# A two-layer attention backbone: attention probabilities transposed by VectorE and DMA through a DRAM scratch

## The chip, the core and the metric

The kernel runs on one core of a Trainium2 chip. The metric is the device time of one execution in microseconds, from from its first to its last instruction with what lies around them. The core's engines work side by side, each through its own queue in order: TensorE (matrix products; in the profile PE for matmuls and PEld for its weight loads), VectorE (DVE), ScalarE (ACT), GpSimd (POOL), and SyncE (SP), which here only issues DMA transfers.

## The reference, cut to what matters

Two layers work on 512 latent tokens and 256 context tokens of width 1024. Layer 0 is differential attention with eight heads; layer 1 is grouped-query attention with eight query heads and two key/value heads.

```python
def sweep_attention(q, k, v):        # for each block of 128 queries
    s = jnp.einsum('bqhgd,bkhd->bhgqk', qblk.astype(jnp.float32), k32) * scale
    p = jax.nn.softmax(s, axis=-1)
    return jnp.einsum('bhgqk,bkhd->bqhgd', p.astype(v.dtype), v)
...
o1 = sweep_attention(qq[..., 0, :], kk[..., 0, :], vv)      # layer 0
o2 = sweep_attention(qq[..., 1, :], kk[..., 1, :], vv)
o = o1 - lam.astype(o1.dtype) * o2
...
o = sweep_attention(qq, kk, vv)                             # layer 1
```

Latent queries read all 768 keys (latent and context). Context queries, in layer 0 alone, read the 256 context keys. Around the attention stand RMS norms, modulation by a condition vector, rotary positions, projections with weights of 1024 columns and gates. The result is the latent stream after both layers, in 32-bit floats.

## The kernel before, in words

**Precision by splitting.** TensorE's products take operands of the type fp32r. To keep 32-bit precision each operand is split into a high part (a copy that rounds to fp32r, on ScalarE) and a low part (the source minus the high part, on VectorE or GpSimd), and each product is three matmuls: high by high, high by low, low by high (`mm3`, line 537).

**Attention, by pairs.** Queries are worked in tiles of 128. A unit (`unit` in `s_units`, line 1267, and in `s1_units`, line 1852) does one tile of one head: TensorE puts 128 x 768 scores into PSUM, VectorE takes the row maximum, ScalarE the exponential with its row sum, VectorE the reciprocal, and GpSimd scales the row (tile `p`). In layer 0 there are two score maps for each tile, and VectorE subtracts the second with `scalar_tensor_tensor`. Two units form a pair, a chunk of 256 queries: two chunks (0 and 1) for each of eight heads in each layer are over latent queries, and layer 0 has a third chunk (2) for each head over context queries.

**The turn.** The product with V needs keys on the partitions, so the probabilities have to be transposed. In `tstep` (lines 1346 and 1879) TensorE transposes blocks of 128 x 128 against the identity matrix, four to a PSUM bank: two key blocks of two query tiles. ScalarE copies the bank into `ah` (high), and VectorE subtracts it from the bank into `al` (low). Three such steps cover 768 keys. In `mstep` (lines 1360 and 1892) `pv_mm` (line 542) runs six matmuls for each step: V's high and low parts stationary, `ah` and `al` moving, 256 columns each. `ah` and `al` have `AB = 3` buffers (line 74). In layer 0 the tile `p` has six buffers, in layer 1 five.

**V and K.** V's projection (`v_mm`, line 1038; `proj_tok`, line 1560, which also serves K and Q of layer 1) has the tokens as its stationary operand, 128 consecutive columns of the activation tiles `hhi`/`hlo` or `h1hi`/`h1lo`, and weights moving, so V comes out with tokens on the partitions. Keys lie with features on the partitions and tokens along the free dimension; `qk_split_` (line 1182) and `k_tr` (line 1739) split them.

**The order of the work.** The program is traced twice. A planner (class `Plan`) first records every operation and its dependences, prices each with constants, and schedules all five queues by list scheduling (`schedule`, line 290): at each step the operation that can start first, ties by priority. Then the program is emitted with exactly these orders, so each queue's order is fixed before the run. For a DMA the planner computes (lines 336 to 338):

```python
go = s + (330 if e == "SP" else 450)
dma = max(dma, go + 300) + op.cost / 350.0
end = max(go + 1700 + op.cost / 350.0, dma) + (800 if op.cost == 131072 else 300)
```

Here `s` is when the queue reaches it, in nanoseconds, and `op.cost` its bytes. Priorities follow from steps with lags (`chunk`, line 763): a transposing step is due 7.0 us (`LA`, line 53) behind its pair's last unit, and its PV step 4.5 us (`LM`, line 73) behind the transposing step. Between these steps the planner fills TensorE with projections of later heads.

**DMA.** SyncE issues weight loads (`wsplit`, line 606) into two `raw` buffers, each 512 KB; ScalarE and GpSimd or VectorE split them. ScalarE's queue issues the small swaps for the rotary positions.

Of the kernel before, what the change touches and what calls it, by code (L numbers as in the profile page):

```python
# [8 lines left out]
F32 = mybir.dt.float32  # L9
# [6 lines left out]
P = 128  # L16
# [31 lines left out]
WBUFS = 3  # L48
XE = [2, 2, 2, 2, 3, 3]
# [24 lines left out]
AB = 3  # L74
MEM = 227168
AHEAD_OPS = 1500
MARGIN = 1.08
SLOT = {}
# [28 lines left out]
class Plan:  # L107


    def __init__(self, mem, psum, sizes):  # L110
        self.mem, self.sizes = mem, sizes
        self.psum = dict(psum)
        self.banks = {t.tensor.name: t.free_size() for t in psum.values()}
        self.width = mem.shape[1]
        self.ops, self.offs, self.tail, self.seen = [], [0], None, {}
        self.marks = []
        self.pools, self.stack = [], {"left": [], "right": []}
        for q in QUEUE:
            setattr(self, q, Queue(self.add, QUEUE[q]))


    def pool(self, name, side="left", psum=False):
        return Pool(self, name, side, psum)

# [41 lines left out]
    def add(self, q, meth, args, kw):  # L166
# [14 lines left out]
        for aps_, w in ((ins, 0), (outs, 1)):  # L181
            for ap in aps_:
                if ap.space == bass.MemoryType.DRAM:
                    continue
                name, spans, parts = self.places(ap)
                if name not in self.banks:
# [103 lines left out]
    def schedule(self, rank):  # L290
# [15 lines left out]
        while len(order) < count:  # L306
# [79 lines left out]
class Emit:  # L386
# [7 lines left out]
    def add(self, eng, meth, args, kw):  # L394
        self.ops.append(getattr(eng, meth)(*args, **kw))  # L395
        return self.ops[-1]

# [81 lines left out]
def tile_backbone(  # L479
# [30 lines left out]
    ps1 = ctx.enter_context(pl.pool("ps1", psum=True))  # L510

# [24 lines left out]

    def mm3(o, ahi, alo, bhi, blo, start, stop):
# [4 lines left out]
    def pv_mm(o, vh, vl, c, ah, al, kt, first, last):  # L542
        terms = [(v, a, e) for v, a in ((vh, ah), (vl, ah), (vh, al)) for e in range(2)]
        for i, (v, a, e) in enumerate(terms):
            nc.tensor.matmul(o, v[:, kt + e, c], a[:, e * 256:e * 256 + 256], start=first and i == 0, stop=last and i == 5)
# [577 lines left out]
    with pl.pool("t0") as t0:  # L1123
# [58 lines left out]
        def qk_split_(h, rr, eng=nc.gpsimd):  # L1182
            qk[h] = tuple(t0.tile([P, T], F32R, tag=f"qk{i}", name=nm("qk"), bufs=1) for i in range(4))
            for r, hi, lo in ((rr[0], *qk[h][:2]), (rr[1], *qk[h][2:])):
                nc.scalar.copy(hi, r)
                eng.tensor_tensor(lo, r, f32(hi), ALU.subtract)
# [77 lines left out]
        def s_units(h, qts):  # L1264
            res = []

            def unit(qt):
# [11 lines left out]
                prev = None  # L1279
                for j in range(nk // w):  # L1280
                    c = slice(k0 + j * w, k0 + j * w + w)
                    for i, (a, b) in enumerate(((qh, kh_), (qh, kl_), (ql, kh_))):
                        for m in (1, 0):
                            r = slice(m * 64, m * 64 + 64)
                            with after(prev), chained(prev):
                                prev = nc.tensor.matmul(
                                    sc[m][:, j if nk == T else m, :w], a[r, tok], b[r, c], start=i == 0, stop=i == 2)
                for m in range(2):
# [3 lines left out]
                    pt = t0.tile([P, T], F32, tag=f"p{m}", name=nm("p"), bufs=6 if m == 0 else 2)[:, :nk]  # L1292
                    pv_ = pt.rearrange("p (j n) -> p j n", j=2) if nk == T else pt
                    nc.scalar.activation(pv_, scv, AF.Exp, bias=mx, accum_out=l[:, m:m + 1])
# [5 lines left out]
                    else:  # L1300
                        nc.vector.tensor_tensor(r, r, nlam, ALU.mult)
                        nc.vector.scalar_tensor_tensor(ps_[0], pt, r, ps_[0], ALU.mult, ALU.add)
                        res.append(ps_[0])

            def unit_ctx():
# [3 lines left out]
                for qt in (NQ, NQ + 1):  # L1309
                    tok = slice(qt * P, (qt + 1) * P)  # L1310
                    for i, (a, b) in enumerate(((qh, kh_), (qh, kl_), (ql, kh_))):
                        for m in (1, 0):
                            r = slice(m * 64, m * 64 + 64)
                            with after(prev), chained(prev):
                                prev = nc.tensor.matmul(
                                    sc[m][:, qt - NQ, :C], a[r, tok], b[r, S:T], start=i == 0, stop=i == 2)
                l = [small(2), small(2)]
                pts = []
                for m in range(2):
                    mx = small(2)  # L1320
                    nc.vector.tensor_reduce(mx, sc[m][:, :, :C], AX.X, ALU.max, negate=True)
                    pt = t0.tile([P, T], F32, tag=f"p{m}", name=nm("p"), bufs=6 if m == 0 else 2)
# [19 lines left out]
        def pv_steps(h, at, ch, after, ts, ms):  # L1342
            kts = range(6) if ch < 2 else range(4, 6)
            st = {}

            def tstep(kt):
                tr = trp()
                for e in range(2):
                    j = kt + e - kts[0]
                    for i, a in enumerate(at):  # L1350
                        nc.tensor.transpose(tr[:, e * 256 + i * P:e * 256 + (i + 1) * P], a[:, j * P:(j + 1) * P], ident)
# [4 lines left out]
                nc.scalar.copy(ah, tr)  # L1356
                nc.vector.tensor_tensor(al, tr, f32(ah), ALU.subtract)
                st[kt] = ah, al

            def mstep(kt):  # L1360
# [6 lines left out]
                pv_mm(o, vh, vl, vc, ah, al, kt, kt == kts[0], kt == kts[-2])  # L1367
                if kt == kts[-2]:
# [5 lines left out]
                    nc.scalar.copy(gT[h][:, sl], o)  # L1374
# [185 lines left out]
    def proj_tok(o, w, t):  # L1560
        sl = slice(t * P, (t + 1) * P)
        for kt in range(KT):
            wh, wl = w[kt // 4]
            c = slice((kt % 4) * 256, (kt % 4) * 256 + 256)
            mm3(o, h1hi[:, kt, sl], h1lo[:, kt, sl], wh[:, c], wl[:, c], kt == 0, kt == KT - 1)
# [127 lines left out]
    with pl.pool("t1", "right") as t1p:  # L1693
# [45 lines left out]
        def k_tr(m, kr):  # L1739
# [4 lines left out]
            sl = slice(m * P, (m + 1) * P)  # L1744
            nc.scalar.copy(kh[:, :, sl], tv)
            nc.vector.tensor_tensor(kl[:, :, sl], tv, f32(kh[:, :, sl]), ALU.subtract)
# [15 lines left out]
        for what, m in KV:  # L1762
# [7 lines left out]
            else:  # L1770
# [3 lines left out]
                run(proj_tok(o, wk if what == "k" else wv, m))  # L1774
# [74 lines left out]
        def s1_units(h, ms):  # L1849
            res = []  # L1850

            def unit(m):
# [4 lines left out]
                for j in range(2):  # L1857
                    c = slice(j * 384, j * 384 + 384)
                    mm3(sc[:, j, :384], qa[:, sl], qb[:, sl], kh[:, g, c], kl[:, g, c], True, True)
# [6 lines left out]
                pt = t1q.tile([P, T], F32, tag="p", name=nm("p"), bufs=5)  # L1866
                l = small()
                nc.scalar.activation(pt.rearrange("p (j n) -> p j n", j=2), scv, AF.Exp, scale=sr, bias=nmx, accum_out=l)
                nc.vector.reciprocal(l, l)
                scaled(EN1, pt, pt, l)  # L1870
                res.append(pt)
# [3 lines left out]
        def pv1_steps(h, at, ch, after, ts, ms):  # L1875
            g = h // 4
            st = {}

            def tstep(kt):
                tr = trp()  # L1880
                for e in range(2):
                    for i, a in enumerate(at):
                        nc.tensor.transpose(tr[:, e * 256 + i * P:e * 256 + (i + 1) * P], a[:, (kt + e) * P:(kt + e + 1) * P], ident)
# [4 lines left out]
                nc.scalar.copy(ah, tr)  # L1888
                nc.vector.tensor_tensor(al, tr, f32(ah), ALU.subtract)
                st[kt] = ah, al  # L1890

            def mstep(kt):
# [5 lines left out]
                pv_mm(o, vh, vl, c, ah, al, kt, kt == 0, kt == 4)  # L1898
                if kt == 4:
                    if ch == 0:  # L1900
                        gT1[h] = t1p.tile([P, 512], F32, tag="g1", name=nm("g1"), bufs=8)
                    (nc.scalar.copy if EG1 == "a" else nc.vector.tensor_copy)(gT1[h][:, ch * 256:ch * 256 + 256], o)
# [217 lines left out]
```

## Time and profile before

| what | us |
| --- | --- |
| median of 3 runs (809.27 to 809.84) | 809.46 |
| the profiled execution's own time | 808.79 |
| its span, first to last instruction | 807.0 |
| TensorE busy (97% of the span) | 786.4 |
| VectorE, ScalarE, GpSimd busy | 473.6, 482.0, 437.4 |
| bytes moved by DMA: 77.78 MB, mean 96 GB/s | |

How to read the rows that follow. A row of a group names the line, the engine, the operation, output <- inputs by the program's names, the shapes and the count; behind the bar stand busy microseconds, mean nanoseconds of one, and the idle time ahead of it with what ended it. Nearly all instructions carry line 395, a helper that emits them, so tiles and operations tell them apart. A row of windows is: stretch, its length, then busy time and count of PE, PEld, DVE, ACT and POOL, the granted TensorE clock, the mean busy share of 16 DMA engines, and GB/s. A row of waits is: who, for whom, microseconds in total, times, longest. A row of DMA issues is: tile <- source, queue, count, KB each, median microseconds from issue to landing. A row of the timeline is: start, length, engine, operation and how many were merged.

### The profile page before, as it was taken

What the parts mean: (1) busy time and instruction counts of PE and PEld (TensorE: products, weight loads), DVE (VectorE), ACT (ScalarE), POOL (GpSimd) and SP (SyncE); (2) the same over time, 40 slices, a digit from 0 to 9 for tenths busy, and PEclk for the clock granted to TensorE, in tenths of its full rate; (3) what the DMA queues carried; (4) which work ended last, traced back from release to release, by engine and by line L of the source; (5) the groups of instructions that cost most, each with busy time, mean ns of one, the idle gap of its engine ahead of it and who ended that gap; (6) DMA issues with size and microseconds to landing.
All of it is one profiled execution on the core that took longest, in us unless ns stands there. A gap on an engine that the chain in (4) does not pass through costs nothing.

```text
span 807.0 us, 14385 instructions
## 1 busy us (share of the span) xinstructions
PE 786.4 (97%) x5482; PEld 699.8 (87%) x5482; DVE 473.6 (59%) x824; ACT 482.0 (60%) x1083; POOL 437.4 (54%) x512
## 2 busy tenths in 40 slices
PE   7899999999999999999999999999999999999997
PEld 5779888889887898797989998898999899898886
DVE  3425787774847546656546743788346455655625
ACT  5524577684565645666538843784466676768622
POOL 4545776874585654757923312366887646644101
PEclk9899999999999999999999999999999999999999
DMA  9951120132142431323430152035321200201112
GB/s 302 363 180 67 65 75 31 40 108 89 40 158 79 144 105 53 105 80 96 165 106 27 62 227 79 1 89 175 120 70 53 96 11 27 79 27 55 51 53 105
DMA packets 41541, 77.78 MB, mean 96 GB/s; under 512 B 3584, under 2 KB 18688, under 8 KB 41472
## 3 DMA queue, kind: packets, MB, share of 16 engines
q1 hardware_dynamic: 38048, 71.71, 27.4%
q10 hardware_dynamic: 3424, 5.15, 1.8%
q8 instruction: 43, 0.70, 0.4%
q14 instruction: 26, 0.21, 0.1%
HBM read 70.56 MB, written 2.10 MB: 90 GB/s over the span
## 4 chain that ended last, share of the span: by engine, by line
PE 91%; DVE 3%; ACT 2%; DMA 2%; issue 1%; SPq 0%; POOL 0%; ACTq 0%; DVEq 0%; POOLq 0%
PE bk L395 75%; PE sc L395 16%; DMA ag<-in_ada_w 1%; DMA raw<-in_post_g 1%; DVE gacc L395 1%; DMA gw<-in_ada_w 0%; ACT whi L395 0%; SPq L395 0%; DVE h L395 0%; ACT sq L395 0%; DVE hf L395 0%; ACT p L395 0%; DVE sw L395 0%; DVE gate L395 0%; ACT jk L395 0%
## 5 line engine op out<-in xcount | busy, mean ns | idle before, releaser
L395 PE MATMUL bk<-whi,h 128*128 128x256 f32 (+1 forms) x1184 | 244.6, 299 | 2.0 <-DVE kn L395 1.3
L395 PE MATMUL bk<-h,whi 128*128 128x512 f32 (+2 forms) x832 | 225.6, 351 | 0.0
L395 POOL TENSOR_TENSOR wlo<-raw,whi 128x256 fp32r<-128x256 f32 x200 | 162.5, 839 | 76.7 <-ACT whi L395 75.3
L395 PEld LDWEIGHTS bk<-whi,h 128*128 128x128 f32 x1184 | 191.0, 189 | 14.6 <-issue 4.9
L395 PE MATMUL bk<-wlo,h 128*128 128x256 f32 (+1 forms) x592 | 176.5, 299 | 0.0
L395 PEld LDWEIGHTS bk<-h,whi 128*128 128x128 f32 x832 | 144.1, 188 | 16.5 <-issue 4.4
L395 PE MATMUL bk<-h,wlo 128*128 128x512 f32 (+2 forms) x416 | 145.7, 351 | 0.0
L395 DVE TENSOR_REDUCE sm<-sc 128x1 f32<-128x768 f32 (+2 forms) x114 | 101.0, 897 | 25.7 <-PE sc L395 25.4
L395 PEld LDWEIGHTS bk<-wlo,h 128*128 128x128 f32 x592 | 111.7, 189 | 4.8 <-issue 1.4
L395 POOL TENSOR_SCALAR p<-p,sm 128x768 f32<-128x768 f32 (+1 forms) x80 | 68.4, 858 | 77.6 <-DVE sm L395 72.8
L395 DVE TENSOR_TENSOR al<-bk,ah 128x512 fp32r<-128x512 f32 x104 | 69.4, 685 | 39.3 <-ACT ah L395 38.8
L395 ACT CAST whi<-raw 128x1024 fp32r<-128x1024 f32 (+1 forms) x70 | 71.7, 1026 | 31.9 <-PE bk L395 27.7
L395 ACT ACTIVATE p<-sc,sm 128x768 f32<-128x768 f32 (+1 forms) x96 | 72.9, 762 | 21.6 <-DVE sm L395 15.6
L395 ACT CAST ah<-bk 128x512 fp32r<-128x512 f32 x104 | 59.0, 590 | 43.5 <-PE bk L395 43.1
L395 PEld LDWEIGHTS bk<-h,wlo 128*128 128x128 f32 x416 | 78.4, 188 | 7.5 <-issue 1.3
L395 PE MATMUL bk<-ident,p 128*128 128x128 f32 x416 | 64.3, 275 | 1.6 <-DVE ql L395 1.1
L395 PEld LDWEIGHTS bk<-ident,p 128*128 128x128 f32 x416 | 49.0, 141 | 11.4 <-issue 2.0
L395 DVE SCALAR_TENSOR_TENSOR p<-p,sm,p 128x768 f32<-128x768 f32 (+1 forms) x48 | 53.4, 1120 | 3.3 <-POOL p L395 0.5
L395 ACT ACTIVATE jk<-bk 128x128 f32<-128x128 f32 (+4 forms) x66 | 22.7, 345 | 53.5 <-PE bk L395 34.4
L395 POOL TENSOR_TENSOR sz<-sz,za 128x384 f32<-128x384 f32 (+1 forms) x24 | 29.4, 1227 | 40.3 <-ACT za L395 39.7
L395 PE MATMUL sc<-qk,qk 64*128 64x384 f32 (+1 forms) x480 | 50.6, 341 | 0.0
L395 DVE RECIPROCAL sm<-sm 128x1 f32<-128x1 f32 (+1 forms) x114 | 18.1, 159 | 52.0 <-ACT p L395 51.5
(191 smaller groups left out, 1375.5 us busy)
## 6 DMA issues: line engine op xcount, KB each, us to landing
raw<-in_a_w SPq DMA_DIRECT2D x30, 512.0 KB, 3.5
araw<-in_ada_w SPq DMA_DIRECT2D x12, 1024.0 KB, 5.3
raw<-in_b_w SPq DMA_DIRECT2D x20, 512.0 KB, 3.5
ag<-in_ada_w SPq DMA_DIRECT2D x32, 256.0 KB, 6.5
raw<-in_w_out SPq DMA_DIRECT2D x16, 512.0 KB, 3.6
sw<-qr ACTq DMA_DIRECT2D x32, 128.0 KB, 2.1
gw<-in_ada_w SPq DMA_DIRECT2D x8, 512.0 KB, 4.1
xt<-in_x SPq DMA_DIRECT2D x4, 512.0 KB, 5.1
```

Source lines behind the costliest of these rows:

```text
L395: self.ops.append(getattr(eng, meth)(*args, **kw))
```

## The change

Chunks 0 and 1 in both layers are turned another way; the context chunk keeps TensorE's transposes. Both units of a pair write their probabilities into one tile `pp` of 1536 elements in each partition, interleaved in runs of 32. VectorE transposes all its 32 x 32 blocks in place with one instruction. Then SyncE stores the tile to a DRAM scratch and loads it back with four transfers that bring the blocks to the right partitions (tile `at`), and ScalarE and VectorE split `ah` and `al` from there, in SBUF. A pair has two buffers of `pp` and two of `at`; `ah` and `al` go from three buffers to two, and the tile `p0` of layer 0 from six of 768 to two of 512.

In the turned tile a partition holds other keys than before: latent tokens t with equal t mod 4, context tokens with equal t mod 2 go together. So V's projections take their stationary tokens with a step of 4 or 2 elements (`keys`), keys are stored permuted (`ordered`, `by_a`) with one more copy and subtraction for each head, context scores read permuted runs of 32 (`by_k`), and PV's moving operand and its output are viewed in runs of 64 and 32. The planner learns of the scratch, prices every DMA issue at 450 ns and adds `DPAD = 500` ns to each landing.

```diff
-AB = 3
+AB = 2
+P0B = 2
+ATB = 2
+PPB = 2
+DRSPLIT = 1
+DRB = 6
+PEWAY = ((), ())
...
-                go = s + (330 if e == "SP" else 450)
+                go = s + 450
                 dma = max(dma, go + 300) + op.cost / 350.0
-                end = max(go + 1700 + op.cost / 350.0, dma) + (800 if op.cost == 131072 else 300)
+                end = max(go + 1700 + op.cost / 350.0, dma) + (800 if op.cost == 131072 else 300) + DPAD
...
+    def keys(src, t):
+        if t < NQ:
+            return src[:, :S].rearrange("p (x k) -> p k x", k=4)[:, t]
+        return src[:, S:].rearrange("p (x k) -> p k x", k=2)[:, t - NQ]
...
+            if moved:
+                d, b = by_a(o, 64), a.rearrange("p (b e x) -> p e b x", b=4, e=2)[:, e]
+            else:
+                d, b = o, a[:, e * 256:e * 256 + 256]
+            nc.tensor.matmul(d, v[:, kt + e, c], b, start=first and i == 0, stop=last and i == 5)
...
+    def turn(pool, pp):
+        flat = pp.rearrange("p b u x -> p (b u x)")
+        nc.vector.transpose(flat, flat)
+        at = pool.tile([P, 4, 384], F32, tag="at", name=nm("at"), bufs=ATB)
+        for lo in range(0, 4, 4 // DRSPLIT):
+            n = 4 // DRSPLIT
+            dr = drp.tile([P // DRSPLIT, 4 * 384], F32, tag="dr", name=nm("dr"), bufs=DRB)
+            nc.sync.dma_start(dr[:, :], flat[32 * lo:32 * (lo + n), :])
+            for q in range(n):
+                nc.sync.dma_start(at[:, lo + q, :], dr[32 * q:32 * q + 32, :].rearrange("j (a c) -> a j c", a=4))
+        return at
+
+    def dma_way(layer, h, ch):
+        return (h, ch) not in PEWAY[layer]
+
+    def split_at(ah, al, src, moved):
+        hi, lo = (by_a(ah, P), by_a(al, P)) if moved else (ah, al)
+        nc.scalar.copy(hi, src)
+        nc.vector.tensor_tensor(lo, src, f32(hi), ALU.subtract)
...
-            sl = slice(t * P, (t + 1) * P)
...
-            mm3(o, hhi[kt][:, sl], hlo[kt][:, sl], wh[:, c], wl[:, c], first and kt == 0, last and kt == KT - 1)
+            mm3(o, keys(hhi[kt], t), keys(hlo[kt], t), wh[:, c], wl[:, c], first and kt == 0, last and kt == KT - 1)
...
                 ah = t0.tile([P, 512], F32R, tag="ah", name=nm("ah"), bufs=AB)
-                nc.scalar.copy(ah, tr)
-                nc.vector.tensor_tensor(al, tr, f32(ah), ALU.subtract)
+                split_at(ah, al, at[0][:, :, kt * 64:kt * 64 + P] if moved else tr, moved)
```

More of the change, by code (lines that the diff above doesn't have):

```diff
@@ L48 @@
 WBUFS = 3
+MEM = 227168
+AHEAD_OPS = 1500
+MARGIN = 1.08
+DPAD = 500
+SLOT = {}
 XE = [2, 2, 2, 2, 3, 3]
@@ L123, in pool, with scratch, dram @@
         return Pool(self, name, side, psum)
+    def scratch(self):
+        self.tile = lambda *args, **kw: self.dram()
+        return nullcontext(self)
+    def dram(self):
+        self.turns += 1
+        return self.drams[(self.turns - 1) % len(self.drams)]
     @contextmanager
@@ L182, in add @@
             for ap in aps_:
-                if ap.space == bass.MemoryType.DRAM:
+                far = ap.space == bass.MemoryType.DRAM
+                if far and all(ap.tensor.name != d.tensor.name for d in self.drams):
                     continue
-                name, spans, parts = self.places(ap)
-                if name not in self.banks:
+                name, spans, parts = (ap.tensor.name, [(0, 2048)], 1) if far else self.places(ap)
+                if name not in self.banks and not far:
                     at = spans[0][0]
@@ L1264, in s_units @@
         def s_units(h, qts):
-            res = []
+            res, pair = [], {}
             def unit(qt):
@@ L1284, in unit @@
                             r = slice(m * 64, m * 64 + 64)
+                            o = sc[m][:, j if nk == T else m, :w]
+                            if moved:
+                                b_ = b[r, j * w:j * w + w]
+                            elif nk == T:
+                                o, b_ = k_a_j(o), by_k(b[r, :], 6)[:, 3 * j:3 * j + 3]
+                            else:
+                                o, b_ = k_a_j(o), by_k(b[r, :], 2)
                             with after(prev), chained(prev):
-                                prev = nc.tensor.matmul(
-                                    sc[m][:, j if nk == T else m, :w], a[r, tok], b[r, c], start=i == 0, stop=i == 2)
+                                prev = nc.tensor.matmul(o, a[r, tok], b_, start=i == 0, stop=i == 2)
+                if nk == T and qt % 2 == 0:
+                    pair[qt // 2] = t0.tile([P, 24, 2, 32], F32, tag="pp", name=nm("pp"), bufs=PPB)
                 for m in range(2):
@@ L1302, in unit @@
                         nc.vector.scalar_tensor_tensor(ps_[0], pt, r, ps_[0], ALU.mult, ALU.add)
-                        res.append(ps_[0])
+                        if not moved:
+                            res.append(ps_[0])
+                        elif qt % 2:
+                            res.append(turn(t0, pair[qt // 2]))
             def unit_ctx():
@@ L1344, in pv_steps @@
             st = {}
+            moved = ch < 2 and dma_way(0, h, ch)
             def tstep(kt):
[L1347 to L1351, printed above, removed]
+                if not moved:
+                    tr = trp()
+                    for e in range(2):
+                        for i, a in enumerate(at):
+                            src = a[:, (kt + e - kts[0]) * P:(kt + e - kts[0] + 1) * P]
+                            nc.tensor.transpose(tr[:, e * 256 + i * P:e * 256 + (i + 1) * P], src, ident)
                 if h == 0 and ch == 0 and kt == 0:
@@ L1564, in proj_tok @@
             c = slice((kt % 4) * 256, (kt % 4) * 256 + 256)
-            mm3(o, h1hi[:, kt, sl], h1lo[:, kt, sl], wh[:, c], wl[:, c], kt == 0, kt == KT - 1)
+            a, b = (keys(t_[:, kt, :], t) if perm else t_[:, kt, sl] for t_ in (h1hi, h1lo))
+            mm3(o, a, b, wh[:, c], wl[:, c], kt == 0, kt == KT - 1)
             yield 3 * 256 / 2400.0
@@ L1743, in k_tr @@
             tv = tr[:, :256].rearrange("p (j n) -> p j n", j=2)
-            sl = slice(m * P, (m + 1) * P)
-            nc.scalar.copy(kh[:, :, sl], tv)
-            nc.vector.tensor_tensor(kl[:, :, sl], tv, f32(kh[:, :, sl]), ALU.subtract)
+            kd = [t.rearrange("p g (a n) -> p g a n", a=4) for t in (kh, kl)]
+            k = 4 if m < NQ else 2
+            for b in range(1 if m < NQ else 2):
+                a, c = (m, slice(0, P)) if m < NQ else (2 * (m - NQ) + b, slice(P, 192))
+                hi, lo = (t[:, :, a, c].rearrange("p g (k j) -> p g k j", k=k) for t in kd)
+                src = tv[:, :, b * 64:b * 64 + 32 * k].rearrange("p g (j k) -> p g k j", k=k)
+                nc.scalar.copy(hi, src)
+                nc.vector.tensor_tensor(lo, src, f32(hi), ALU.subtract)
         def k_rope(m, o, r):
@@ L1773, in tile_backbone @@
                 o = pj(256)
-                run(proj_tok(o, wk if what == "k" else wv, m))
+                run(proj_tok(o, wk if what == "k" else wv, m, what == "v"))
                 if late:
@@ L1865, in unit @@
                 nc.scalar.activation(nmx, mx, AF.Copy, scale=sr)
-                pt = t1q.tile([P, T], F32, tag="p", name=nm("p"), bufs=5)
+                if m % 2 == 0:
+                    pair[0] = t1q.tile([P, 24, 2, 32], F32, tag="pp", name=nm("pp"), bufs=PPB)
+                if moved:
+                    pt = unit_view(pair[0], m % 2)
+                    pv_, src = pt.rearrange("p (j b) x -> p j b x", j=2), scv.rearrange("p j (b x) -> p j b x", x=32)
+                else:
+                    pt = unit_row(pair[0], m % 2)
+                    pv_, src = pt.rearrange("p (j n) -> p j n", j=2), scv
                 l = small()
-                nc.scalar.activation(pt.rearrange("p (j n) -> p j n", j=2), scv, AF.Exp, scale=sr, bias=nmx, accum_out=l)
+                nc.scalar.activation(pv_, src, AF.Exp, scale=sr, bias=nmx, accum_out=l)
                 nc.vector.reciprocal(l, l)
                 scaled(EN1, pt, pt, l)
-                res.append(pt)
+                if not moved:
+                    res.append(pt)
+                elif m % 2:
+                    res.append(turn(t1q, pair[0]))
             return res, [Step(lambda m=m: unit(m), 0.97) for m in ms]
@@ L1877, in pv1_steps @@
             st = {}
+            moved = dma_way(1, h, ch)
             def tstep(kt):
[L1880 to L1883, printed above, removed]
+                if not moved:
+                    tr = trp()
+                    for e in range(2):
+                        for i, a in enumerate(at):
+                            src = a[:, (kt + e) * P:(kt + e + 1) * P]
+                            nc.tensor.transpose(tr[:, e * 256 + i * P:e * 256 + (i + 1) * P], src, ident)
                 if h == 0 and ch == 0 and kt == 0:
@@ L2107 @@
             mem = mp.tile([P, MEM // 4], F32, name="mem")[:]
+            drams = [drp.tile([P // DRSPLIT, 4 * 384], F32, name=f"dr{i}")[:, :] for i in range(DRB)]
             sizes, pl = None, None
             while pl is None or sizes != pl.sizes:
-                pl = Plan(mem, psum, sizes)
+                pl = Plan(mem, psum, drams, sizes)
                 tile_backbone(pl, *args)
```

85 lines of the change are left out of this document (59 added, 26 removed).

## The prediction, as it was put on record

> **What bounds the kernel now.** I read the busy shares first, then the chain that ended last, then what TensorE waited for, then the two attention stretches by windows.
>
> ```profile
> PE 786.4 (97%) x5482; PEld 699.8 (87%) x5482; DVE 473.6 (59%) x824; ACT 482.0 (60%) x1083; POOL 437.4 (54%) x512
> ...
> PE 91%; DVE 3%; ACT 2%; DMA 2%; issue 1%; SPq 0%; POOL 0%; ACTq 0%; DVEq 0%; POOLq 0%
> ```
> ```profile
> PE sc L395 <- POOL xt L395: 2.5, 1, 2.5
> PE bk L395 <- DVE al L395: 1.8, 2, 1.4
> ```
> ```profile
> 83.00:262.00 179.00, 178.91 (x1243) 153.27 (x1242) 125.68 (x197) 114.97 (x244) 121.66 (x118) 1.00 0.23 74
> 262.00:440.00 178.00, 177.60 (x1281) 156.29 (x1281) 104.61 (x183) 106.88 (x228) 101.41 (x102) 1.00 0.30 97
> 593.00:745.00 152.00, 149.85 (x1046) 140.78 (x1046) 83.53 (x159) 105.18 (x244) 93.02 (x117) 1.00 0.15 49
> ```
>
> TensorE is 97% busy and carries 91% of the chain; its longest single wait is 2.5 us, and for split probabilities (al) it waits 1.8 us in the whole run. Layer 0's attention runs from 83 to 440 us, layer 1's from 593 to 745. In both TensorE has no gap, VectorE is 65% and 55% busy, and the sixteen DMA engines average 0.27 and 0.15. So an instruction that leaves TensorE there shortens the run, as long as nothing else comes later than it does now.
>
> **What the change removes.** The transposes of probabilities:
>
> ```profile
> L395 PE MATMUL bk<-ident,p 128*128 128x128 f32 x416 | 64.3, 275 | 1.6 <-DVE ql L395 1.1 <-DVE al L395 0.4
> ```
> ```profile
> 639.99 0.60 PE L395 MATMUL bk<-ident,p 128*128 128x128 f32 x4
> ...
> 642.06 0.40 PE L395 MATMUL bk<-ah,vh 128*128 128x256 f32 x2
> ```
>
> The 275 ns is a latency; four in a row take 0.60 us, so one follows another after (0.60 - 0.275) / 3 = 0.108 us. Eight heads, two layers, two chunks of 256 queries, twelve transposes each: 384 go (the context chunk keeps 32). That is 384 x 0.108 = **41.5 us**, half of it, 20.7, in each layer. The matmuls that stay are taken at their pace of now (256 columns: 0.12 us), except those in the third point below.
>
> **What it adds, where something already covers it.** VectorE turns 32 pairs, 1536 elements in each partition. No such instruction is in the trace; the nearest rows are one-input instructions:
>
> ```profile
> L395 DVE TENSOR_REDUCE sm<-sc 128x1 f32<-128x768 f32 x96 | 90.3, 949 | 24.9 <-PE sc L395 24.6
> ...
> L395 DVE TENSOR_TENSOR al<-bk,ah 128x512 fp32r<-128x512 f32 x104 | 69.4, 685 | 39.3 <-ACT ah L395 38.8
> L395 DVE SCALAR_TENSOR_TENSOR p<-p,sm,p 128x768 f32<-128x768 f32 x32 | 41.8, 1307 | 2.3
> ...
> L395 DVE TENSOR_TENSOR sw<-sw,rope 128x512 f32<-128x512 f32 x16 | 18.2, 1137 | 1.6 <-DMA sw<-qr 1.6
> ...
> L395 DVE TENSOR_TENSOR h<-hf,h 128x512 fp32r<-128x512 f32 x20 | 15.7, 791 | 4.6 <-ACT h L395 4.0 <-POOL hf L395 0.6
> ...
> L395 DVE TENSOR_REDUCE sm<-sc 128x2 f32<-128x512 f32 x14 | 9.1, 680 | 0.9 <-PE sc L395 0.9
> ...
> L395 DVE TENSOR_SCALAR xt<-xt,sm 128x1024 f32<-128x1024 f32 x5 | 4.2, 843 | 11.2 <-POOL sm L395 11.1
> ```
>
> A reduce costs (949 - 680) / 256 = 1.05 ns an element, so a turn costs 949 + 768 x 1.05 = 1.76 us. The ends are 1.26 (TENSOR_SCALAR's 843 ns scaled to 1536) and 2.6 (twice the 1307). I take 1.76, since a transposer reads one stream and has no second tensor. Second, 96 subtractions for al now read both inputs from SBUF: 791 to 1137 ns in place of 685; I take +0.2 us near the lower row, the same operation on the same types. Third, ScalarE's splits also read SBUF, a few hundredths each.
>
> In layer 0 VectorE goes from 230 to about 230 + 16 x 1.76 + 48 x 0.2 = 268 of 336 us: covered by TensorE. In layer 1 it goes from 84 to 84 + 28 + 10 = 122 of the 131 us that TensorE would need. That is 93%, in a stretch where every pair's max, turn and split follow one another, so I charge 8 us there (0 to 14) if nothing else sets layer 1. The smaller buffers (two of each split for three, two pairs, two turned pairs) cost nothing while a turned tile is held under two of layer 1's 9.5 us periods; it is held about 10 us for landing and 5 for three splits. Splitting the keys in two pieces (an extra ScalarE and GpSimd instruction for each head) lies beside 0.6 busy shares and costs nothing; without that cover it is 8 x 0.4 us.
>
> **The transfers.** Each pair's turned tile is stored (768 KB) and loaded back in four pieces (192 KB each), all five issued by SyncE, in order. The store waits for VectorE, the first load waits for the store to land, and the three others and every weight load stand behind it on that queue.
>
> ```profile
> raw<-in_a_w SPq DMA_DIRECT2D x30, 512.0 KB, 3.5
> araw<-in_ada_w SPq DMA_DIRECT2D x12, 1024.0 KB, 5.3
> ...
> ag<-in_ada_w SPq DMA_DIRECT2D x32, 256.0 KB, 6.5
> ...
> out_x<-u SPq DMA_DIRECT2D x6, 256.0 KB, 2.1
> ...
> out_x<-u SPq DMA_DIRECT2D x2, 128.0 KB, 1.8
> ```
> ```profile
> 20.00:40.00 20.00, 17.91 (x105) 14.09 (x105) 9.25 (x15) 12.04 (x21) 11.59 (x17) 0.83 1.08 363
> ```
> ```profile
> 641.90 0.93 SPq L395 DMA_DIRECT2D raw<-in_b_w  x2
> ```
>
> The store: out_x grows by 0.3 us for 128 KB, so 2.1 + 4 x 0.3 = 3.3 us; midway between the loads of 512 and 1024 KB is 4.4. The loads: an issue takes 0.47 us, a piece between 1.8 and 2.1 us like out_x, so the last lands after 3 x 0.47 + 2.0 = 3.4 us, or 4.4 with some queueing, if each is dealt over all sixteen engines. The planner, whose constants stand in the code, allows 5.2 for the store (0.45 + 1.7 + 786432 / 350 ns + 0.8) and 4.9 for the loads, 10.1 in all. By these rows it allows enough.
>
> But the four loads have a shape that no transfer of before has. Their source walks four column blocks outermost, 32 rows inside each; every transfer of before has at least 64 rows outermost. Nothing shows such a pattern on sixteen engines. In the full window sixteen engines move 363 GB/s, 22.7 GB/s each. On four engines, the same four for every piece, 786432 / 4 bytes each take 8.7 us, and with the 1.4 us that out_x's 1.8 leaves beside its bytes (8 KB an engine at 22.7 is 0.36) the last piece lands after 10.1 us. The bounds are 3.4 and 10.1. I take the far end, because the code's source pattern offers four parts and not sixteen.
>
> [...]
>
> So a pair takes 1.8 + 3.9 + 10.1 us, about 4 us more than planned. **Layer 0** has a pair every 22 us, so four busy engines (16 x (8.7 + 2.2) + 0.27 x 357 = 271 of 357 us) keep up; what hurts is lateness. ScalarE's split stands in order in its queue: late by 4, it holds the exponentials and evacuations behind it. In the plan the PV matmuls stand 4.5 us (LM) behind the split, which itself needs 0.6 + 0.7 on the two engines, so some 3 of the 4 us are covered: 16 x 1 = 16 us lost (0 if the next pair covers the rest, 62 if nothing is covered). **Layer 1** has a pair every 9.5 us, and there the four engines need 8.7 + 2.2 = 10.9 us for its bytes alone: 16 x 10.9 = 174, and 12 us for the first scores and the last PV, makes 186 against 152. That is **+34** where -20.7 was to be had (with 0.15 x 152 = 23 us of other transfers on those engines +57; with spread loads -12.7).
>
> **Strided weight loads.** V's projections now take every fourth (latent) or second (context) token as the stationary operand: 576 matmuls in layer 0 and 144 in layer 1, 480 of them with steps of 16 bytes.
>
> ```profile
> L395 PEld LDWEIGHTS bk<-h,whi 128*128 128x128 f32 x832 | 144.1, 188 | 16.5 <-issue 4.4
> ```
>
> All rows of before are contiguous, 188 ns of latency, hidden behind a pace of 0.12 us. I take 0 for the stride, with 480 x 0.1 = 48 us as the other end: a load of twice 0.108 in place of 0.117. Below zero it can't go, as the same columns are loaded.
>
> [...]
>
> **Sum.** From the profiled execution's 808.8 (span 807.0 and 1.8 around it): - 20.7 + 16 in layer 0, + 34 in layer 1: 838.1. The median shown is 0.7 above that execution, so 838.8, say **839 us**. The forecast alone lies between 815 and 890.
>
> **Rivals.**
> 1. *Hidden (faster).* The four loads are spread over the engines, or land inside the plan's 10.1 us. Then the chain's work is covered, layer 0 gives 20.7 and layer 1 20.7 - 8: 808.8 - 33.4 + 0.7 = **776 us** (766 to 792). For it: no waits now, DMA shares of 0.27 and 0.15, and rows that give 6.7 to 8.8 us for store and loads. Against it: the source's shape, and layer 1's 93% on VectorE. It decides as soon as loads land within about 5 us.
> 2. *The stationary operand's stride (slower).* Transfers hidden as in 1, but V's strided loads run at half pace: 776 + 48 = **824 us**. It turns the sign from a pace of 0.19 us for those 480 on (33 / 480 = 0.07 above 0.12). For it: TensorE loads weights 87% of the time and has no slack in those stretches. Against it: nothing but the lack of a row.
> 3. *Both, or weight loads starved behind waiting stores on SyncE's queue,* **above 890 us**: the queue already waits 194.5 us for buffers, so I give it little.
>
> ```profile
> SPq L395 <- ACT whi L395: 194.5, 27, 20.9
> ```
>
> **Chances.** Forecast 0.42, hidden 0.33, stride 0.18, above 890 0.05, no change 0.02. A measurement of this kernel tells about 0.2% from no change. Faster by more than that 0.33, within it 0.02, slower 0.65. The range must hold the forecast, the stride and about two thirds of the hidden case: 773 to 890. The likeliest sign's own range is 815 to 890.
>
> **What would show it.** 32 transposes of p left and 32 VectorE transposes of about 1.76 us; the loads of at landing after 10 us (forecast) or under 5 (hidden); TensorE waiting for al or ah, ScalarE and VectorE waiting for the loads; in layer 1 a pair every 11 us and a DMA share that four engines explain. For the stride: 256-column matmuls of V's projections 0.2 us apart. The prediction is wrong if the loads land early, or if late loads move nobody.

## The result and the profile after

The changed kernel takes **962.68 us** (median of 4 runs, 960.75 to 962.86) against 809.37 us before (4 runs): a ratio of **1.1888 [1.1867, 1.1908]**. The forecast was 839 us with a range up to 890. The sign was right, the size was not.

The profiled execution of the changed kernel spans 960.9 us. First the page: busy times, the granted clock in 40 slices, and the chain that ended last.

```profile
span 960.9 us, 14024 instructions
...
PE 848.0 (88%) x5098; PEld 751.9 (78%) x5098; DVE 524.4 (55%) x859; ACT 488.5 (51%) x1093; POOL 444.7 (46%) x519
...
PEclk9999999899987999799999999999988878798899
...
DMA 14%; PE 5%; DVE 2%; SPq 1%; ACT 1%; issue 1%; POOL 0%; DVEq 0%; ACTq 0%
```

TensorE runs 384 instructions fewer (5482 to 5098) and is nevertheless busy 62 us longer and idle 92 us longer. The chain, which reaches back only into layer 1 here, is led by DMA, where before TensorE carried 91%.

The groups that answer to the change (all instructions carry line 411 now):

```profile
L411 DVE STREAM_TRANSPOSE pp<-pp 128x1536 f32<-128x1536 f32 x32 | 56.6, 1768 | 2.8 <-POOL pp L411 2.8
...
L411 PE MATMUL bk<-ident,p 128*128 128x128 f32 x32 | 5.4, 294 | 0.4 <-DVE gate L411 0.4
```
```profile
L411 PEld LDWEIGHTS bk<-whi,h 128*128 128x128 f32 x1184 | 234.2, 230 | 18.0 <-issue 4.9 <-DVE kn L411 2.5 <-DVE tb L411 1.6
```

The turn costs VectorE 1.77 us, and 32 TensorE transposes are left. The third row is the group of weight loads that holds V's projections: 230 ns on the mean. The same group in the kernel before:

```profile
L395 PEld LDWEIGHTS bk<-whi,h 128*128 128x128 f32 x1184 | 191.0, 189 | 14.6 <-issue 4.9 <-DVE kn L395 1.6 <-DVE kl L395 0.8
```

The waits, in all and those of TensorE:

```profile
POOL pp L411 <- DVE sm L411: 114.3, 33, 10.2
DVE al L411 <- ACT ah L411: 107.9, 47, 6.7
ACT ah L411 <- DMA at<-dr: 85.3, 22, 7.4
...
PE bk L411 <- ACT ah L411: 64.4, 18, 5.8
```

ScalarE's split waits 85 us for loads and TensorE 64 us for the split; before, TensorE waited 1.8 us for split probabilities. Windows of layer 0's attention, the stretch between, and layer 1's attention:

```profile
83.00:500.00 417.00, 380.08 (x2292) 327.44 (x2292) 247.60 (x377) 216.90 (x455) 234.43 (x228) 0.95 0.38 127
500.00:684.00 184.00, 176.11 (x1161) 166.51 (x1160) 106.34 (x196) 102.15 (x275) 72.45 (x105) 0.98 0.33 109
684.00:930.00 246.00, 188.96 (x1052) 171.75 (x1051) 126.69 (x198) 123.90 (x275) 99.79 (x120) 0.85 0.41 139
```

In layer 1 TensorE is idle for 57 of 246 us and its granted clock is 0.85; it was 1.00 before.

**A table by stage** says more than any total. Its bounds are the first exponential of a layer (written to `pp`, before to `p`) and the last start of a PV matmul with `al`, read from the views of the tiles `pp` (before: `p`) and `al`, where the two times of a row are the first and the last start. Before and after:

```profile
L395 ACT ACTIVATE p<-sc,sm x96: 462/899/928, 83.2 to 438.4; 128x768 f32<-128x768 f32 x64, 128x256 f32<-128x256 f32 x32
...
L395 ACT ACTIVATE p<-sc,sm,qrs x32: 973/994/1020, 593.1 to 738.8; 128x768 f32<-128x768 f32 x32
```
```profile
L395 PE MATMUL bk<-al,vhi x112: 277/280/388, 103.4 to 465.8; 128*128 128x256 f32 x112
L395 PE MATMUL bk<-al,vh x96: 277/280/367, 609.8 to 761.2; 128*128 128x256 f32 x96
```
```profile
L411 ACT ACTIVATE pp<-sc,sm x32: 886/900/912, 91.4 to 496.9; 128x768 f32<-128x768 f32 x32
...
L411 ACT ACTIVATE pp<-sc,sm,qrs x32: 972/992/1011, 684.4 to 897.0; 128x768 f32<-128x768 f32 x32
```
```profile
L411 PE MATMUL bk<-al,vhi x112: 274/281/415, 125.4 to 542.6; 128*128 128x256 f32 x112
...
L411 PE MATMUL bk<-al,vh x96: 277/370/415, 710.7 to 927.1; 128*128 128x256 f32 x96
```

| us, profiled executions | start | layer 0 | between | layer 1 | tail | span |
| --- | --- | --- | --- | --- | --- | --- |
| before | 83.2 | 382.6 | 127.3 | 168.1 | 45.8 | 807.0 |
| after | 91.4 | 451.2 | 141.8 | 242.7 | 33.8 | 960.9 |
| e1, V's operand contiguous | 80.7 | 422.2 | 130.9 | 244.4 | 33.2 | 911.4 |
| e2, loads with 32 rows outermost | 91.9 | 411.6 | 141.8 | 172.3 | 33.2 | 850.8 |
| e3, both | 81.0 | 375.5 | 130.9 | 170.6 | 33.2 | 791.2 |

Start, "between" and layer 0 tell of the stride (e1 against after); layers 0 and 1 tell of the loads (e2 against after). The tail shrinks whenever layer 1 goes through the scratch, because work moves ahead of the last PV matmul: in e3, 83 matmuls fewer than before start in the tail and, transposes aside, 83 more in layer 1. So layer 1 and tail have to be read together.

### The profile page after: what moved, and what is told of

Same layout as the page of the kernel before. It is cut to its first block, busy times and chain, and to the rows that moved or that the text cites. A ratio compares the mean times of both kernels' runs of the same rounds, so it can differ in the third digit from the quotient of the medians.

```text
span 960.9 us, 14024 instructions
## 1 busy us (share of the span) xinstructions
PE 848.0 (88%) x5098; PEld 751.9 (78%) x5098; DVE 524.4 (55%) x859; ACT 488.5 (51%) x1093; POOL 444.7 (46%) x519
## 5 line engine op out<-in xcount | busy, mean ns | idle before, releaser
L411 PE MATMUL bk<-whi,h 128*128 128x256 f32 (+1 forms) x1184 | 290.0, 332 | 4.2 <-DVE kn L411 2.2
L411 PEld LDWEIGHTS bk<-whi,h 128*128 128x128 f32 x1184 | 234.2, 230 | 18.0 <-issue 4.9
L411 DVE TENSOR_TENSOR al<-at,ah 128x512 fp32r<-128x512 f32 x96 | 76.5, 813 | 120.4 <-ACT ah L411 107.3
L411 PEld LDWEIGHTS bk<-wlo,h 128*128 128x128 f32 x592 | 136.0, 230 | 5.4 <-issue 1.6
L411 POOL TENSOR_SCALAR pp<-pp,sm 128x768 f32<-128x768 f32 x64 | 62.3, 973 | 129.9 <-DVE sm L411 114.3
L411 ACT CAST ah<-at 128x512 fp32r<-128x512 f32 x96 | 57.4, 617 | 113.7 <-DMA at<-dr 85.3
L411 PE MATMUL bk<-ah,vh 128*128 128x256 f32 x96 | 27.9, 384 | 55.7 <-ACT ah L411 55.7
L411 DVE STREAM_TRANSPOSE pp<-pp 128x1536 f32<-128x1536 f32 x32 | 56.6, 1768 | 2.8 <-POOL pp L411 2.8
L411 PEld LDWEIGHTS sc<-qk,qk 64*128 64x128 f32 x480 | 38.9, 188 | 14.2 <-issue 5.2
L411 ACT ACTIVATE p<-sc,sm 128x768 f32<-128x768 f32 (+1 forms) x64 | 43.9, 687 | 6.9 <-DVE sm L411 5.3
L411 ACT ACTIVATE jk<-bk 128x128 f32<-128x128 f32 (+4 forms) x66 | 22.8, 346 | 45.8 <-PE bk L411 26.0
```

## The experiments

The theory after the result: two independent costs, the step of 16 bytes in V's stationary operand, and loads that only four DMA engines carry. The rival to each: it is the other one alone, or the longer chain as such. The kernel before ran again beside each set of runs, with medians from 806.9 to 807.7 us; the ratios go by these.

**e1_natural: V's stationary operand contiguous again.** Another order of the keys gives the same turn with consecutive tokens as the operand. (The order in which K is stored changes with it.)

```diff
-            return src[:, :S].rearrange("p (x k) -> p k x", k=4)[:, t]
-        return src[:, S:].rearrange("p (x k) -> p k x", k=2)[:, t - NQ]
+            return src[:, t * P:(t + 1) * P]
+        return src[:, t * P:(t + 1) * P]
```

> V's stationary tokens contiguous again (another key order, the same transfers). Theory (two separate costs: four-engine loads, and weight loads that run at half pace with a step of 16 bytes, 480 x 0.117 us = 56 us): 48 us less where TensorE is the bound, some of it swallowed by waits for the loads: 905 to 925 us, and no weight load of V above 0.2 us. Rival (the late loads set everything, the slow weight loads fill time that would be waited anyway): 950 us or more.

Measured 914.02 us, ratio to before 1.1308 [1.1273, 1.1344]: 48.7 us less than after. The weight loads are at 190 ns again, and TensorE waits for `ah` as long as it did:

```profile
PE bk L411 <- ACT ah L411: 64.1, 19, 6.8
PE bk L411 <- DMA araw<-in_ada_w: 12.3, 2, 8.4
PE bk L411 <- ACT sqs L411: 8.2, 4, 4.7
PE sc L411 <- ACT p L411: 7.6, 1, 7.6
PE bk L411 <- ACT sz L411: 4.6, 1, 4.6
```

So the stride is a cost of its own and not a face of the late loads. The timeline of TensorE in the changed kernel shows it one instruction at a time (start, length): contiguous up to 73.58, strided from 73.69 on.

```profile
73.34 0.40 PE L411 MATMUL sc<-h,whi 128*128 128x256 f32 x2
73.58 0.28 PE L411 MATMUL sc<-h,wlo 128*128 128x256 f32 x1
73.69 0.40 PE L411 MATMUL bk<-whi,h 128*128 128x256 f32 x1
73.93 0.40 PE L411 MATMUL bk<-wlo,h 128*128 128x256 f32 x1
74.17 0.63 PE L411 MATMUL bk<-whi,h 128*128 128x256 f32 x2
74.63 0.40 PE L411 MATMUL bk<-wlo,h 128*128 128x256 f32 x1
```

From 73.69 to 74.63 four matmuls start 0.235 us apart; a contiguous one takes 0.12 (73.34 to 73.58 for two). That is 0.115 us for each of 480, 55 us.

**e2_spread: the same bytes in four loads with 32 rows outermost,** so that each fills 32 partitions of `at` with all four blocks.

```diff
-            for q in range(n):
-                nc.sync.dma_start(at[:, lo + q, :], dr[32 * q:32 * q + 32, :].rearrange("j (a c) -> a j c", a=4))
+            for a in range(4):
+                nc.sync.dma_start(at[32 * a:32 * a + 32, lo:lo + n, :], dr[:, a * 384:a * 384 + 384].rearrange("(q j) c -> j q c", j=32))
```

> The same bytes loaded by four transfers of 32 partitions each, with 32 rows outermost in source and destination instead of four blocks; strides as in the changed kernel. Theory (loads confined to four of sixteen engines): a set of loads lands about 5 us after the store instead of 10, TensorE hardly waits for ah, 825 to 850 us. Rival (the round trip through DRAM and the one queue are late anyway): still about 9 us and above 930 us.

Measured 851.19 us, 1.0531 [1.0494, 1.0568]: 111.5 us less than after, and 1 us above the theory's range. The page's rows of DMA issues (KB each, median us to landing) and TensorE's wait:

```profile
dr<-pp SPq DMA_DIRECT2D x32, 768.0 KB, 3.9
at<-dr SPq DMA_DIRECT2D x128, 192.0 KB, 4.3
```
```profile
PE bk L411 <- ACT ah L411: 4.5, 4, 1.5
```

How busy the engines are can be read from the views. In the changed kernel packets of 1536 bytes are these loads alone; three to five of them are under way in 282 of the 315 us in which any is, and never more than eight. From 769.5 to 771.5 us, with nothing else under way, the mean busy share of the sixteen engines is 0.24, and 91 GB/s are moved. In e3, whose loads are those of e2, it is 0.78 and 173 GB/s from 598.5 to 602 us, between the loads' issue and SyncE's next one. By these shares (0.24 x 16 = 3.8, 0.78 x 16 = 12.5) an estimate is that about four engines carry the loads in the one and twelve or more in the other.

In the changed kernel its chain of waits, between 744 and 800 us, shows loads of 10 us and stores of 5.0 and 9.6:

```profile
745.62 1.78 DVE pp L411
...
747.42 4.96 DMA dr<-pp
...
754.08 9.96 DMA at<-dr
...
764.19 0.63 ACT ah L411
...
764.86 1.24 PE bk L411 x4
...
766.12 0.63 ACT ah L411
...
766.77 0.69 DVE al L411
767.46 0.33 DVE sm L411
...
768.49 0.93 POOL pp L411
...
769.45 1.78 DVE pp L411
...
771.26 9.62 DMA dr<-pp
...
782.58 9.47 DMA at<-dr
```

This is also how lateness spreads in layer 1. In VectorE's queue the subtraction for `al` (766.77), late because of the load, stands ahead of the reciprocal (`sm`) of the next softmax; behind that come GpSimd's scaling (768.49), the next turn (769.45), the next store (771.26). The rows give the loop: load 10.0, split and subtraction 3.3, softmax and turn 3.8, store 9.6, issues of the next loads 1.7, in all 28.5 us from the loads at 754.08 to those at 782.58. Another pair's loads begin in between (768.4), so that is two pairs, 14.25 us each. GpSimd's waits for `sm` belong here in part: they are 114 us in all, 73 before and 61 in e3. The long stores (9.6 us, where the median in e2 is 3.9) would fit a share of each store that waits behind loads on four busy engines, which is the author's guess. Of the store at 771.26, three quarters of the packets are through 2.0 us after the first began, the last one 8.3 us after it, while the loads that began at 768.4 run until 778.5. The trace doesn't name the engine of a packet, so that they share engines is not shown.

Measured, for the same bytes: about 10 us to landing with four blocks outermost (9.96 and 9.47 above), 4.3 us with 32 rows outermost. The two also fill the partitions of `at` in another way, and no run parts the one from the other.

**e3_both: both edits.**

> Contiguous stationary tokens and loads with 32 rows outermost together. Theory: both costs gone, what is left is the 41.5 us of transposes less what VectorE's 93% in layer 1 takes back: 772 to 800 us, faster than the 809 of before. Rival (VectorE, the one transfer queue or the smaller buffers cost as much as the transposes): 805 to 860.

Measured 796.67 us (792.98 to 800.44), ratio **0.9872 [0.9838, 0.9906]**: faster than both kernels. The two savings, 48.7 and 111.5, add up to 160 of the 166 us. So stride and loads explain the whole loss, and the idea of the change gains 11 us once they are mended (807.65 before, beside it). Its windows, in layer 0 and layer 1:

```profile
83.00:440.00 357.00, 346.43 (x2363) 296.05 (x2362) 265.83 (x397) 222.94 (x482) 237.05 (x228) 0.99 0.52 158
...
593.00:760.00 167.00, 157.46 (x1003) 142.26 (x1002) 129.15 (x189) 118.54 (x263) 100.85 (x113) 1.00 0.70 202
```

TensorE, almost without a gap before, is now idle 10.6 us in the first and 9.5 us in the second. The question left: 41.5 us of transposes went, 11 us came out. Where is the rest?

**e4_tensore: the changed kernel with 30 of the 32 pairs turned by TensorE,** strides and small buffers kept (the lists stand here in words). It parts stride and buffers from the transfers.

```diff
-PEWAY = ((), ())
+PEWAY = (all pairs but (3, 0), all pairs but (3, 0))
```

> The changed kernel with its stride and permuted keys, but 30 of 32 pairs turned by TensorE as before. Theory: 809 plus 480 x 0.117 = 56 us, so 855 to 875. Rival (the stride costs only in the company of DMA traffic or a lower clock): 808 to 820.

Measured 877.43 us, 1.0856 [1.0823, 1.0888], 2 us above the theory's range: 70 us lost with two pairs of transfers left. Its timeline also has V's context tokens, whose step is 8 bytes:

```profile
67.05 0.28 PE L411 MATMUL sc<-h,wlo 128*128 128x256 f32 x1
67.17 0.28 PE L411 MATMUL bk<-whi,h 128*128 128x256 f32 x1
67.29 0.28 PE L411 MATMUL bk<-wlo,h 128*128 128x256 f32 x1
67.41 0.41 PE L411 MATMUL bk<-whi,h 128*128 128x256 f32 x2
```

They start 0.12 us apart, as contiguous ones do (73.34 to 73.58 above). So only the 480 with a step of 16 bytes, 0.235 us apart, pay, by the count above 55 of the 70 us; e11 has the rest.

**e5_late: the changed kernel, each load priced 5.2 us later by the planner,** so that its order expects the landing that really comes.

```diff
-... + DPAD
+... + DPAD + (5200 if op.cost == 196608 else 0)
```

> The changed kernel with one edit in its planner: each of the four loads is priced 5.2 us later, as they land. Theory (four engines cost twice: lateness against the order, which a true price mends, and their throughput in layer 1, which it can't mend): layer 0 gets 15 to 35 us back, layer 1 stays above 220 us, 925 to 950 us. Rival (only the order written for earlier loads is wrong): near the 851 of the spread loads, 850 to 880.

Measured 950.26 us, 1.1765 [1.1739, 1.1791]: 12 us less than after, of 111 that shorter loads give. Layer 0 got 9.1 us back, less than the theory's 15 to 35, and layer 1 stayed at 232.3, as it said. The order was not the main thing, as far as one price for the loads can tell.

**e8_layer0 and e9_layer1: e3 with one layer turned by TensorE again** (`PEWAY` names all pairs of the other layer).

> Contiguous stationary tokens, spread loads, and layer 1 turned by TensorE again: layer 0 alone by VectorE and DMA. Theory (layer 0 gives its 20.7 us of transposes, layer 1 loses by the change because every queue there is near full): 780 to 790 us, faster than the 797 with both layers. Rival (both layers give the same share): 800 to 806.

Measured 806.91 us (12 runs), 0.9993 [0.9978, 1.0008]. The expected 780 to 790 were missed, and the rival's range by 1 us: the theory that layer 1 loses on the new way fell.

> The same two edits, but layer 0 turned by TensorE and layer 1 by VectorE and DMA. Theory: slower than before by 5 to 15 us, 813 to 823. Rival: faster than before, 796 to 804.

Measured 811.77 us, 1.005 [1.0032, 1.0067], between the two ranges. By stages, layer 1 with its tail takes 202.4 us where before took 213.9: layer 1 gains 11.5. What loses is layer 0, on TensorE's own way: 393.4 where before took 382.6. It does there what the kernel before did, but with the small buffers and with scores that read permuted keys.

**e10_best: e8 with three split buffers in layer 1** (`AB` 2 in layer 0, 3 in layer 1).

> As the run with layer 0 alone, and the split buffers of layer 1 back at three. Theory (the third buffer lets the split run ahead of PV, as before): 2 to 5 us less than with two. Rival (TensorE is the bound in layer 1 with two as well): within 1 us of it.

Measured 809.93 us (12 runs), 1.0019 [0.9999, 1.0039]: nothing gained there, and 3 us more than e8, outside both ranges.

**e11_small, e12_two, e13_third: the small buffers alone.** e11 is e3 with all but one pair of each layer turned by TensorE. e12 is the kernel before with `AB = 2`. e13 is e9 with three split buffers in layer 0 (and seven scratch tiles for six).

> Contiguous V operands and loads over 32 rows as in the best version (797 us), but only one pair in each layer ((2,0)) goes through the scratch; the other 30 are turned by TensorE, with the change's small buffers. Theory: the small buffers themselves cost the TensorE way about 11 us, nearly all of it in layer 0 (first exponential to last PV 393 where before has 383): 815 to 822. Rival: they cost nothing, and what layer 0 lost with TensorE's way came from the neighbourhood of layer 1's transfers: 805 to 811. Either way the difference to the same kernel with strided V operands and slow loads (877) is 56 for the stride and a few us for two slow pairs.

> The kernel before with one thing changed that matters: two buffers of ah and al in place of three (the probabilities keep their six and five; four of the 17 warming matmuls at the very start are left out so that the start is at most 1 us other). Theory (the third split buffer is what the TensorE way lacked): 814 to 822. Rival (the missing tiles of probabilities are it, six for two pairs): 806 to 810.

> Layer 0 turned by TensorE, layer 1 through the scratch with both mends (811.8), now with three split buffers in layer 0. Theory (third split buffer): layer 0 gets back its 10.8 us, 799 to 804. Rival (probabilities' tiles): 809 to 813.

e11 measured 824.86 us, 1.0209 [1.0186, 1.0232], against 807.4 before: TensorE's way in the changed kernel is 17 us slower (layer 0 takes 392.1 for 382.6, between 133.1 for 127.3), above the 815 to 822 of the theory; the rival is out. These 17 us are not the buffers alone: e11 also has the permuted keys, the new planner's prices and two pairs through the scratch. Against e4 it is 52.6 us less: the stride once more, and two pairs' slow loads. e12 measured 812.22 us, 1.0056 [1.0036, 1.0075], between the two ranges: two split buffers cost the kernel before 4.8 us. e13 measured **800.87 us, 0.9898 [0.9877, 0.9918]**: the third split buffer gives 10.9 us back, as the theory said, and layer 0 takes 382.9 us, as before, with the permuted keys still there. Windows of layer 0, e9 and then e13:

```profile
83.00:440.00 357.00, 348.13 (x2434) 300.73 (x2434) 206.45 (x348) 207.77 (x447) 213.88 (x221) 0.99 0.25 86
```
```profile
83.00:440.00 357.00, 356.75 (x2523) 309.88 (x2521) 220.86 (x374) 219.71 (x475) 224.24 (x227) 1.00 0.27 86
```

With two buffers TensorE is idle 8.9 us of 357 and does 2434 matmuls; with three it is idle 0.25 us and does 2523.

**e14_three: e3 with three split buffers in layer 0, paid for by one loaded tile `at` there in place of two.**

> The best version so far (both mends, all 32 pairs through the scratch, 797 us), with three split buffers in layer 0; one buffer of the loaded tile there in place of two pays for them. Theory: the third split buffer gives layer 0 what it gave TensorE's way, part or all of 11 us: 786 to 793. Rival: on the way through the scratch the splits wait for loads and not for buffers, and a single loaded tile makes the loads of the next pair wait for three splits, with weight loads behind them: 796 to 806.

Measured 822.84 us, 1.0186 [1.0161, 1.0212], 26 us more than e3: the rival's mechanism, at a price above its range. Layer 0 takes 405.4 us for e3's 375.5, and ScalarE waits for loads again, 34.7 us for e3's 10.7, once for 10.6:

```profile
ACT ah L411 <- DMA at<-dr: 34.7, 12, 10.6
```

A second loaded tile is worth more there than a third split buffer. Three split buffers beside two loaded tiles weren't tried. e3 keeps the lowest median; its interval overlaps e13's.

## Why the prediction was wrong, point by point

Three steps failed. The stride was put at nothing, the late loads in layer 0 were sized at 16 us, and layer 1 was taken at the pace of four engines where a loop of waits was slower. That it came out slower was forecast, and for one of the two reasons.

**What it removes:** right in count; 384 transposes went. But even with both costs mended only 11 of the 41.5 us came out (below).

**VectorE:** right. The turn takes 1.768 us for 1.76; the subtraction for `al` 0.813 for 0.885 (0.934 in e3).

**The transfers, far end taken:** right in kind. The loads land about 10 us after their issue, as 10.1 said, and spreading them was worth 111.5 us. That four blocks in the source mean four engines was the author's estimate; no view names an engine, and what fits it is the busy share of 0.24 with these loads alone.

**Layer 0, +16 of 0 to 62:** mis-sized. The loads cost layer 0 46.7 us (422.2 in e1 against 375.5 in e3). The step that failed is "some 3 of the 4 us are covered". TensorE is idle 47.0 us in e1's layer 0 and 10.6 in e3's. By e1's rows above, it waits there for other results of ScalarE (`sqs`, `p`, `sz`: 20.4 us), as the prediction feared, and in that window 8.2 us for the split. It also waits 12.3 us, against 1.3 in e3, for weights (`araw`) that come by the same queue as the stores and loads; the forecast had nothing for that, only rival 3 named it.

**Layer 1, +34:** the failed reading is that four engines' throughput, 10.9 us a pair, sets the pace. The first packets of the sixteen sets of loads lie 14.4 us apart (696.7 to 912.6 us). Four engines would not have been full: in 61 of the window's 246 us fewer than four data packets of any transfer were under way. The loop of load, split, subtraction, softmax, turn and store decided, with its 28.5 us for two pairs. Against before, layer 1 and tail lost 276.5 - 213.9 = 62.6 us.

**"I take 0 for the stride":** failed, and by itself it is about the distance from the forecast to the end of its range. 480 loads at 0.115 us more make 55 us, and taking the stride out gave 48.7; the far end of 48 that the prediction kept was it. Its twice 0.108 = 0.216 us a matmul was an estimate that no row of before showed; the changed kernel's timeline shows 0.235. It belonged to the forecast as well as to a rival: stride and loads don't exclude each other, and rival 3, "both", with 0.05, is what happened. All ends together, 839 + 48 for the stride, + 46 in layer 0, + 23 in layer 1, make 956 us: the range took in one bad end at a time. That 956 is so near the 963 is in part luck, since the end for layer 1 stood on the wrong reason and the small buffers were not in it.

**Smaller buffers "cost nothing":** failed. Its reason was about the turned tile alone. Two split buffers for three cost 4.8 us in the kernel before and 10.9 in e9.

**Rival 1, 776 us:** its mechanism and its point were right: with loads at 4.3 us TensorE waits 4.5 us (e2) and not 64 for the split. e3 spans 791.2 us, 793.0 with what lies around it, where rival 1 without its 0.7 for the median says 775.4; this is e3's fastest execution, its median is 796.7. By stages against before: start -2.2, layer 0 -7.1, between +3.6, layer 1 and tail -10.1. Layer 1 gave about what was forecast (-12.7). Layer 0 gave little of its 20.7: transposes aside, 18 matmuls fewer than before start in it and 21 more in the stretch between, and the two together gave 3.5 us. On TensorE's way two split buffers cost layer 0 10.5 us (e9 against e13); that they cost the new way as much would fit its 10.6 us idle, but no run shows it, since e14 had to give up a loaded tile. Why the stretch between grows stays open in part: it does by 3 to 6 us in e3, e8, e9 and e11 with 21 to 28 more matmuls, but also by 3.4 in e13 with none more.

## What to carry to other kernels

Before a transfer is priced by its bytes, look at the pattern it walks: here 768 KB landed after 10 us with four blocks outermost and after 4.3 us with 32 rows, and the change turned from 19% slower to 1% faster with that and a contiguous stationary operand. Unknown costs that can occur together have to be added at their far ends before the range is drawn, not shared out among rivals. And a buffer count is part of the price: whatever pays for a new tile's room must be asked what it covered.

## What the runs showed of the hardware beside that

V's matmuls of 256 columns started 0.12 us apart with a step of 8 bytes in the stationary operand (e4, 67.17 to 67.41), as with a contiguous one (the changed kernel, 73.34 to 73.58), and 0.235 us apart with a step of 16 bytes (73.69 to 74.63). No run shows why, and none has another step.

The granted clock was 0.85 in the changed kernel's layer 1, with 57 of 246 us idle, and 1.00 in layer 1 of e3, with 9.5 of 167. Idle time does not settle it: from 20 to 40 us the kernel before was granted 0.83 with TensorE busy for 17.9 us, the changed kernel 1.00 with 18.7. The median PV matmul with `al` in layer 1 takes 370 ns in the changed kernel and 280 in e3; that the clock is the cause is not shown.
